# A hybrid decoder layer: the second parts of twelve weight splits, by accumulating transfers instead of GpSimd subtractions

## The chip, the cores and the metric

The kernel runs on one core of one Trainium2 chip. The metric is the device time of one execution in microseconds (us). The engines are PE (TensorE; PEld are its weight loads), DVE (VectorE), ACT (ScalarE), POOL (GpSimd) and SP (SyncE, which here only issues transfers). Transfers run on 16 DMA engines; SP, ACT and POOL can issue them.

## The reference

One decoder layer on 1024 tokens of width 1024, all in float32. A first projection of the normalised input is cut into the parts of four gated delta-rule heads (key, query, value of 128 columns each, an output gate `dz`, a decay and a beta for each token) and of four differential-attention heads. The outputs of both groups go through `w_out`, and a gated feed-forward block with a short causal convolution follows.

```python
proj = rms_norm(h, norm1_w[l]) @ w_in[l]
dq, dk, dv, dz, da, db, fq, fk, fv = jnp.split(proj, IN_SPLITS, axis=-1)
qkv = jax.nn.silu(causal_dwconv(jnp.concatenate([dq, dk, dv], axis=-1), dn_conv_w[l]))
...
o_a = gated_delta_rule(q_a, k_a, v_a, g_a, beta_a).astype(h.dtype)
o_a = rms_norm(o_a, dn_norm_w[l]) * jax.nn.silu(dz.reshape(B_, S_, DN_HEADS, DN_HEAD_V))
...
h = h + mix @ w_out[l]
u = causal_dwconv(rms_norm(h, norm2_w[l]) @ w_up[l], ffn_conv_w[l], ffn_conv_b[l])
gate, up = jnp.split(u, 2, axis=-1)
h = h + (jax.nn.silu(gate) * up) @ w_down[l]
```

## The kernel before, in words

PE multiplies in a reduced form of float32 (fp32r). To keep float32's accuracy every large operand x is split in two: the high part is x copied into that form, the low part is x minus the high part. A product is then three matmuls: high by high, high by low and low by high.

`split_w` (L200) makes the two parts of a tile of weights that has been loaded into a raw buffer (`raw`, three buffers in turn). ACT writes the high part (L202, `whi`), and then POOL (L204) or DVE (L206) subtracts it from the raw weights and writes the low part (`wlo`). Both parts come from one pool of five buffers (`wt`), which the splits take in turn: high, low, high, low, and so on. So a low part's buffer is the one that held the high part two splits earlier, and it comes free when PE has read that for the last time.

`gemm_T` (L415) computes one projection of a delta head, transposed: 128 columns of `w_in` against all 1024 tokens, in two halves of 512 tokens, each 8 times L422, L423 (high part of the weights) and L424 (low part), 48 matmuls in all. Its sums (`gT`, two PSUM buffers) are copied out by ACT at L433 (`pT`). `proj_T` (L429) calls it for the key (kind 1), the query (0) and the value (2) of each of the four heads. Key and query of head 0 are split earlier, while the input is normalised. `proj_nat` (L383 to L411) computes 256 columns untransposed; one call makes the second half of the gate, `dz`, from two raw tiles, each with four of the eight rows of blocks of the weights: L403 and L404 with the high parts, then L406 with the low parts.

The heads are worked one behind the other. While head h is prepared (`delta_prep`: decay `dec`, four-tap convolutions L573 with their activation L575, transposes `pk` L611 and `pv` L657, score products `pkk` and `pkq` L638, L639, which DVE masks at L643, L645), inverted (`delta_inverse`, L684 to L743) and scanned (`delta_scan`: `pP`, `pzz`, `pS`, `po`, with DVE steps `s` between them), PE fills its gaps with the projections of the next head. POOL has, beside the subtractions, causal masks (L594, L673), a product with the decay (L647) and one with the gate (`szh`, L791).

No order is written out by hand for this stage. A scheduler sets each engine's order when the program is built, from priorities given by `part(...)` and from its own estimates of durations; afterwards every engine runs its instructions strictly in that order, and an instruction that waits holds up all behind it. Transfers issued by SP stand in SP's order in the same way; a raw buffer's next load waits until its last reader is done.

Of the kernel before, what the change touches and what calls it, by code (L numbers as in the profile page):

```python
# [10 lines left out]
F32 = mybir.dt.float32  # L11
# [3 lines left out]
AF = mybir.ActivationFunctionType  # L15
ALU = mybir.AluOpType
AX = mybir.AxisListType

P = 128
# [39 lines left out]
def hybrid_layer(ctx, tc, x, positions, norm1_w, w_in, dn_conv_w, dn_a_log, dn_dt_bias,  # L59
# [2 lines left out]
                 ffn_conv_b, w_down, cst, out, dbg=None, stop=None):  # L62
    nc = tc.nc
    V, S, G, PE = nc.vector, nc.scalar, nc.gpsimd, nc.tensor
    dbg = dbg or {}

    cp = ctx.enter_context(tc.tile_pool(name="cp", bufs=1))
# [14 lines left out]
    @contextmanager  # L82
    def part(name):
        p = tc.cur_priority
        q = max(0, p - PRI[name])
        tc.cur_priority = q
        yield
        tc.cur_priority = p + tc.cur_priority - q
# [3 lines left out]
    def nm(s):  # L92
        uid[0] += 1
        return f"{s}_{uid[0]}"
# [4 lines left out]
    def gtr(s):  # L99
        return gt(s, dt=F32R)  # L100

    def jt(s, dt=F32):
        return jp.tile([P, T], dt, tag="j", name=nm(s))

    def ct_(s, dt=F32):
        return cq.tile([P, T], dt, tag="c", name=nm(s))
# [13 lines left out]
    def psG(s="pG"):  # L120
        return pq.tile([P, 512], F32, tag="G", name=nm(s), bufs=2)
# [16 lines left out]
    win = w_in.rearrange("l d c -> (l d) c")  # L138
# [61 lines left out]
    def split_w(raw, lo_eng=None, w=T, alloc=None):  # L200
        hi, lo = ((alloc or wt)(s)[:, 0:w] for s in ("whi", "wlo"))
        S.activation(hi, raw[:, 0:w], AF.Copy)  # L202
        if lo_eng is G:
            G.tensor_tensor(lo, raw[:, 0:w], hi.bitcast(F32), op=ALU.subtract)  # L204
        else:
            V.tensor_tensor(lo, raw[:, 0:w], hi.bitcast(F32), op=ALU.subtract)  # L206
        return hi, lo

    def load_w128(w, c0, lo_eng=None, after=None):

        raw = rp.tile([P, T], F32, tag="raw", name=nm("raw"))
        if after is not None:
            G.tensor_copy(raw[:, 0:1], after)
        nc.sync.dma_start(raw.rearrange("p (k c) -> p k c", c=P),
                          w[:, c0:c0 + P].rearrange("(k p) c -> p k c", p=P))
        hi, lo = split_w(raw, lo_eng)
        return (hi.rearrange("p (k c) -> p k c", c=P), lo.rearrange("p (k c) -> p k c", c=P))

    def load_wn(srcs, lo_eng=None, kg=4, alloc=None, after=None):


        wd = sum(w for _, _, w in srcs)
        parts = []
        for k0 in range(0, NK, kg):
            n = min(kg, NK - k0)
            raw = rp.tile([P, T], F32, tag="raw", name=nm("raw"))
            if after is not None:
                V.tensor_copy(raw[:, 0:1], after)
            rv = raw[:, 0:n * wd].rearrange("p (k c) -> p k c", c=wd)
            o = 0  # L230
            for w, c0, w_ in srcs:
                nc.sync.dma_start(
                    rv[:, :, o:o + w_],
                    w[k0 * P:(k0 + n) * P, c0:c0 + w_].rearrange("(k p) c -> p k c", p=P))
                o += w_
            hi, lo = split_w(raw, lo_eng, n * wd, alloc)
            parts.append((hi.rearrange("p (k c) -> p k c", c=wd),
                          lo.rearrange("p (k c) -> p k c", c=wd)))
        return lambda kt: (parts[kt // kg][0][:, kt % kg, :], parts[kt // kg][1][:, kt % kg, :])
# [39 lines left out]
    def new_xn():  # L279

        return [tuple(xp.tile([P, 4 * T], F32R, tag="xn", name=nm("xn")) for _ in range(2))
                for _ in range(2)]

    def xs(xn, part, kt, a, b):
        q = a // 512
        return xn[q][part][:, kt * 512 + a - q * 512:kt * 512 + b - q * 512]
# [13 lines left out]
    xn = new_xn()  # L300
# [3 lines left out]
    with tc.manual_schedule(engines={mybir.EngineType.Activation}):  # L304
        for tt in range(NT + 1):
# [7 lines left out]
            if 0 < tt < 4:  # L313
                k = tt - 1
                n = min(3, NK - 3 * k)
                hi, lo = (gtr("w0")[:, 0:n * 264].rearrange("p (k c) -> p k c", c=264) for _ in range(2))
# [70 lines left out]
    def proj_nat(srcs, dst, lo_eng=None, extra=None):  # L387


        wf = load_wn(srcs, lo_eng, 4) if extra is None else lambda kt: tuple(t[:, kt % 3, :] for t in srcs[kt // 3])  # L390
        npt = 1 if extra is not None else 2
        for q in range(2):
            st = jt("pn")
            for t0 in range(0, 4, npt):
                ps = psG("pn")
                for i in range(npt):
                    tt = q * 4 + t0 + i
                    a, b = tt * P, tt * P + P
                    w = 264 if extra is not None else 256
                    o = ps[:, i * w:(i + 1) * w]  # L400
                    for kt in range(NK):
                        wh, wl = wf(kt)
                        PE.matmul(o, xs(xn, 0, kt, a, b), wh, start=kt == 0, stop=False)  # L403
                        PE.matmul(o, xs(xn, 1, kt, a, b), wh, start=False, stop=False)  # L404
                    for kt in range(NK):
                        PE.matmul(o, xs(xn, 0, kt, a, b), wf(kt)[1], start=False, stop=kt == NK - 1)  # L406
                if extra is not None:
                    V.tensor_copy(extra[:, tt, :], ps[:, 256:264])
                S.activation(st[:, t0 * 256:(t0 + npt) * 256], ps[:, 0:npt * 256], AF.Copy)
                yield  # L410
            nc.sync.dma_start(  # L411
                pn_dram[q * 512:(q + 1) * 512, dst:dst + 256].rearrange("(t p) c -> p t c", p=P),
                st.rearrange("p (t c) -> p t c", c=256))

    def gemm_T(w, c0, x_, ps, lo_eng, qq=(0, 1)):  # L415

        whi, wlo = pre.pop(c0 // P, None) or load_w128(w, c0, lo_eng)
        for q in qq:
            qs = (q * 512, q * 512 + 512)
            o = ps(q)  # L420
            for kt in range(NK):
                PE.matmul(o, whi[:, kt, :], xs(x_, 0, kt, *qs), start=kt == 0, stop=False)  # L422
                PE.matmul(o, whi[:, kt, :], xs(x_, 1, kt, *qs), start=False, stop=False)  # L423
                PE.matmul(o, wlo[:, kt, :], xs(x_, 0, kt, *qs), start=False, stop=kt == NK - 1)  # L424
            yield q, o
# [3 lines left out]
    def proj_T(h, kind):  # L429
        ct = kind * 4 + h  # L430
        st = praw[ct] = ct_("pT")
        for q, o in gemm_T(win, ct * P, xn, lambda q: psG("gT"), G):
            S.activation(st[:, q * 512:(q + 1) * 512], o, AF.Copy)  # L433
            yield

    def steps(gen, n=99):
        for _ in range(n):
            if next(gen, gen) is gen:
                break

    nat0 = proj_nat(wf0, 0, extra=dab)
    head0 = [proj_T(0, kind) for kind in (1, 0, 2)]
    steps(nat0, 4)
    steps(head0[0], 1)
# [18 lines left out]
    for bits in (8, 8, 8):  # L463
        e = math.floor(math.log2(abs(rest)))
        q = 2.0 ** (e - bits + 1)
# [115 lines left out]
    def load_rows(h):  # L581
        dec = gt("dec")
        nc.sync.dma_start(dec, G_dram[h:h + 1, :].broadcast_to([P, T]))
        return dec
# [387 lines left out]
    def delta_proj(h):  # L972
        for kind in (1, 0, 2):
            steps(proj_T(h, kind))

    def delta_end(d):
        with part("dscan"):
            delta_scan(d)
        with part("dout"):
            delta_out(d)  # L980

    ds_ = []
    for h in range(4):
        dec = load_rows(h)
        if h > 0:
            with part("dproj"):
                delta_proj(h)
            if h == 3:
                with part("dz1"):
                    steps(proj_nat([(win, 1792, 256)], 256, G))  # L990
        with part("dprep"):
            ds_.append(delta_prep(h, dec))
        if h > 0:
            delta_end(ds_[h - 1])
        with part("dinv"):
            delta_inverse(ds_[h])
# [15 lines left out]
    def load_wo(k0, c, eng, alloc=None):  # L1012

        parts = []
        for i in range(2):
            raw = rp.tile([P, T], F32, tag="raw", name=nm("raw"))
            r0 = (k0 + 2 * i) * P
            nc.sync.dma_start(raw.rearrange("p (k c) -> p k c", c=512),
                              wout[r0:r0 + 2 * P, c * 512:(c + 1) * 512].rearrange("(k p) c -> p k c", p=P))
            parts.append(split_w(raw, eng, T, alloc))  # L1020
        return lambda k: tuple(t[:, (k % 2) * 512:(k % 2) * 512 + 512] for t in parts[k // 2])
# [379 lines left out]
```

## Time and profile before

| | us |
|---|---|
| median of 3 runs | 1429.41 (1425.66 to 1430.79) |
| the profiled execution | 1430.1 |
| its span, first to last instruction | 1428.4 |
| PE busy in the span | 1334.5 |
| DVE, ACT, POOL busy | 878.3, 611.3, 377.0 |

The profiled execution is 0.7 us above the median of the runs. Busy times are sums over the whole span; since the stages of the kernel have different limits, a change in one stage is read from that stage's rows. In a row with square brackets, the bracket holds the time that the engine sat idle just before, and the instruction whose end released it. PE's clock is the one that the chip granted, as a share of full speed.

### The profile page before, as it was taken

The numbers are of one execution on the slowest core, as the hardware profiler recorded it, in microseconds if no ns is written. First come the engines' busy times: TensorE is split into PE (matmuls) and PEld (weight loads), VectorE is DVE, ScalarE is ACT, GpSimd is POOL, SyncE is SP. The second block draws the span as 40 slices with busy tenths as digits, with TensorE's granted clock in tenths as the row PEclk, the third lists the DMA queues.
The fourth block names the chain that finished last, engine by engine and source line by source line (L and its number), as shares of the span: only waits on it lengthen the run. The fifth ranks groups of instructions, "written<-read, shape, count | busy, mean of one in ns | idle before, by whom it ended". The sixth has DMA issues, their size and how long they took to land. (4 is left out here: it accounts for less than half of the span.)

```text
span 1428.4 us, 20608 instructions
## 1 busy us (share of the span) xinstructions
PE 1334.5 (93%) x7927; PEld 1126.6 (79%) x7927; DVE 878.3 (61%) x1745; ACT 611.3 (43%) x1086; POOL 377.0 (26%) x295
## 2 busy tenths in 40 slices
PE   7998898989989998999887999999999989999998
PEld 6876676888989986778665788888888868888887
DVE  5467978886342368867787666666666656334321
ACT  6445454533325365665554444444444435222220
POOL 3044313131242245240022434444333420000000
PEclk8999999999999999999998999999999999999999
DMA  7231112031543267455331222222222247547421
GB/s 225 83 80 35 34 39 75 17 113 66 162 109 116 88 169 192 105 134 162 123 121 29 89 74 89 85 78 89 89 74 82 82 137 243 195 149 229 139 88 59
DMA packets 143393, 155.14 MB, mean 109 GB/s; under 512 B 9279, under 2 KB 114367, under 8 KB 143295
## 3 DMA queue, kind: packets, MB, share of 16 engines
q1 hardware_dynamic: 130815, 144.14, 31.8%
q0 software_dynamic: 11008, 8.39, 3.1%
q8 instruction: 62, 1.02, 0.3%
q10 hardware_dynamic: 1472, 1.29, 0.3%
q14 instruction: 36, 0.29, 0.1%
HBM read 111.32 MB, written 38.29 MB: 105 GB/s over the span
## 5 line engine op out<-in xcount | busy, mean ns | idle before, releaser
L385 PE MATMUL pd<-whi,gl 128*128 128x512 f32 x352 | 137.0, 389 | 0.0
L383 PE MATMUL pd<-whi,gh 128*128 128x512 f32 x352 | 137.0, 389 | 0.0
L384 PE MATMUL pd<-wlo,gh 128*128 128x512 f32 x352 | 137.0, 389 | 0.0
L204 POOL TENSOR_TENSOR wlo<-raw,whi 128x1024 fp32r<-128x1024 f32 x34 | 83.8, 2471 | 194.1 <-PE gT L424 68.2
L1316 POOL TENSOR_TENSOR acc<-acc,acc 128x1024 f32<-128x1024 f32 x22 | 53.6, 2437 | 243.8 <-issue 215.5
L403 PE MATMUL pn<-whi,xn 128*128 128x256 f32 x448 | 116.3, 293 | 0.0
L404 PE MATMUL pn<-whi,xn 128*128 128x256 f32 x448 | 115.4, 291 | 0.0
L1339 ACT ACTIVATE gh<-act 128x1024 fp32r<-128x1024 f32 x42 | 44.6, 1061 | 123.9 <-PE pd L384 100.2
L1340 DVE TENSOR_TENSOR gl<-act,gh 128x1024 fp32r<-128x1024 f32 x42 | 52.0, 1241 | 68.9 <-ACT gh L1339 68.6
L403 PEld LDWEIGHTS pn<-whi,xn 128*128 128x128 f32 x448 | 87.3, 195 | 0.3
L404 PEld LDWEIGHTS pn<-whi,xn 128*128 128x128 f32 x448 | 87.0, 195 | 0.1
L202 ACT ACTIVATE whi<-raw 128x1024 fp32r<-128x1024 f32 x58 | 61.0, 1052 | 52.1 <-issue 18.3
L206 DVE TENSOR_TENSOR wlo<-rx,whi 128x1024 fp32r<-128x1024 f32 x22 | 28.9, 1315 | 82.6 <-ACT whi L202 82.3
L424 PE MATMUL gT<-xn,wlo 128*128 128x512 f32 x192 | 79.3, 413 | 0.0
L1230 PE MATMUL pa<-xT,whi 128*128 128x512 f32 x176 | 70.5, 400 | 9.3 <-ACT xT L1103 5.3
L422 PE MATMUL gT<-xn,whi 128*128 128x512 f32 x192 | 78.8, 410 | 0.0
L423 PE MATMUL gT<-xn,whi 128*128 128x512 f32 x192 | 78.6, 409 | 0.0
L202 ACT ACTIVATE whi<-rx 128x1024 fp32r<-128x1024 f32 x22 | 23.3, 1061 | 127.4 <-POOL rx L1271 127.4
L383 PEld LDWEIGHTS pd<-whi,gh 128*128 128x128 f32 x352 | 66.1, 188 | 13.8
L385 PEld LDWEIGHTS pd<-whi,gl 128*128 128x128 f32 x352 | 66.1, 188 | 13.7
L384 PEld LDWEIGHTS pd<-wlo,gh 128*128 128x128 f32 x352 | 66.1, 188 | 13.6
L206 DVE TENSOR_TENSOR wlo<-raw,whi 128x1024 fp32r<-128x1024 f32 x24 | 29.4, 1225 | 72.3 <-PE pd L384 53.1
(377 smaller groups left out, 3765.9 us busy)
## 6 DMA issues: line engine op xcount, KB each, us to landing
act<-act_dram SPq DMA_DIRECT2D x42, 512.0 KB, 4.5
rw<-in_w_up_dram SPq DMA_DIRECT2D x22, 512.0 KB, 3.8
act_dram<-acc SPq DMA_DIRECT2D x22, 512.0 KB, 2.6
raw<-in_w_down_dram SPq DMA_DIRECT2D x22, 512.0 KB, 4.4
raw<-in_w_in_dram SPq DMA_DIRECT2D x18, 512.0 KB, 4.0
pn_dram<-pn SPq DMA_DIRECT2D x16, 512.0 KB, 3.4
rx<-in_w_up_dram SPq DMA_DIRECT2D x22, 256.0 KB, 2.8
rz<-in_w_up_dram SPq DMA_DIRECT2D x22, 256.0 KB, 3.3
```

Of the source, the lines that this page charges most:

```text
L202: S.activation(hi, raw[:, 0:w], AF.Copy)
L204: G.tensor_tensor(lo, raw[:, 0:w], hi.bitcast(F32), op=ALU.subtract)
L206: V.tensor_tensor(lo, raw[:, 0:w], hi.bitcast(F32), op=ALU.subtract)
L383: PE.matmul(ps, lh, rh, start=first, stop=False)
L384: PE.matmul(ps, lh, rl, start=False, stop=False)
L385: PE.matmul(ps, ll, rh, start=False, stop=last)
L403: PE.matmul(o, xs(xn, 0, kt, a, b), wh, start=kt == 0, stop=False)
L404: PE.matmul(o, xs(xn, 1, kt, a, b), wh, start=False, stop=False)
L422: PE.matmul(o, whi[:, kt, :], xs(x_, 0, kt, *qs), start=kt == 0, stop=False)
L423: PE.matmul(o, whi[:, kt, :], xs(x_, 1, kt, *qs), start=False, stop=False)
L424: PE.matmul(o, wlo[:, kt, :], xs(x_, 0, kt, *qs), start=False, stop=kt == NK - 1)
L1230: PE.matmul(ps, wh[:, ks], xh[k], start=first, stop=False, skip_group_check=not start)
```

## The change

`split_w` gets a third way to make the low part: ACT writes the negated high part into the low part's buffer (a copy with scale -1), and a transfer issued by POOL adds the raw weights to it where they lie. `proj_T` and the projection of the gate's second half choose it. `proj_T`'s choice applies to ten projections: the value of head 0 and all three of heads 1 to 3; key and query of head 0 have been split before, by a call that still names POOL. With the gate's two tiles that is twelve splits. All others keep their engine.

```diff
+    DMA = nc.sync
...
     def split_w(raw, lo_eng=None, w=T, alloc=None):
         hi, lo = ((alloc or wt)(s)[:, 0:w] for s in ("whi", "wlo"))
         S.activation(hi, raw[:, 0:w], AF.Copy)
-        if lo_eng is G:
+        if lo_eng is DMA:
+
+            S.activation(lo, raw[:, 0:w], AF.Copy, scale=-1.0)
+            G.dma_start(lo.bitcast(F32), raw[:, 0:w], accum_op=ALU.add)
+        elif lo_eng is G:
             G.tensor_tensor(lo, raw[:, 0:w], hi.bitcast(F32), op=ALU.subtract)
...
-        for q, o in gemm_T(win, ct * P, xn, lambda q: psG("gT"), G):
+        for q, o in gemm_T(win, ct * P, xn, lambda q: psG("gT"), DMA):
...
-                    steps(proj_nat([(win, 1792, 256)], 256, G))
+                    steps(proj_nat([(win, 1792, 256)], 256, DMA))
```

`DMA` is only a name for the choice; the transfers are issued by POOL. Lines behind the edit are five higher in the changed kernel (L422 is L427 there).

The scheduler's orders move with it. On ACT, where head 0's value is split and head 1's key begins, the order before was this (`gT` and `pT` are the projections of head 0; the numbers tell buffers apart):

```order
L433 ACTIVATE pT_98_545<-gT_107_710 128x512 [waits PE_49]
L202 ACTIVATE whi_153_1251<-raw_152_1249 128x1024 [waits DMAHW7_49,Pool_49]
L790 ACT_TABLE_LOAD
L790 ACTIVATE szh_256_1707<-szh_256_1707 128x1024 [waits DMAHW4_49]
L790 ACTIVATE szh_373_2398<-szh_373_2398 128x1024 [waits DMAHW5_49]
L433 ACTIVATE pT_103_628<-gT_108_736 128x512 [waits PE_49]
L202 ACTIVATE whi_159_1310<-raw_158_1308 128x1024 [waits DMAHW1_49,Pool_49]
L433 ACTIVATE pT_109_762<-gT_113_769 128x512 [waits PE_49]
L433 ACTIVATE pT_109_762<-gT_114_795 128x512 [waits PE_49]
```

On ACT at the same place now:

```order
L206 ACTIVATE wlo_112_766<-raw_110_763 128x1024 [waits PE_49,Pool_49]
L438 ACTIVATE pT_98_545<-gT_107_710 128x512 [waits PE_49]
L203 ACTIVATE whi_153_1252<-raw_152_1250 128x1024 [waits DMAHW7_49]
L795 ACT_TABLE_LOAD
L795 ACTIVATE szh_256_1711<-szh_256_1711 128x1024 [waits DMAHW4_49]
L795 ACTIVATE szh_373_2405<-szh_373_2405 128x1024 [waits DMAHW5_49]
L438 ACTIVATE pT_103_628<-gT_108_736 128x512 [waits PE_49]
L206 ACTIVATE wlo_154_1253<-raw_152_1250 128x1024 [waits Pool_49]
L203 ACTIVATE whi_159_1312<-raw_158_1310 128x1024 [waits DMAHW1_49]
L438 ACTIVATE pT_109_762<-gT_113_770 128x512 [waits PE_49]
L206 ACTIVATE wlo_160_1313<-raw_158_1310 128x1024 [waits PE_49,Activation_49]
L438 ACTIVATE pT_109_762<-gT_114_796 128x512 [waits PE_49]
```

Three copies into low parts' buffers have come in, each with the wait for that buffer, ahead of evacuations of projections.

On PE, at the first transposes `pk` of head 0's key, which stand between matmuls of head 1's query (`gT_162`), the order before was this:

```order
L422 MATMUL gT_162_1340<-xn_16_140,whi_159_1310 128x512
L423 MATMUL gT_162_1340<-xn_17_141,whi_159_1310 128x512
L424 MATMUL gT_162_1340<-xn_16_140,wlo_160_1311 128x512
L422 MATMUL gT_162_1340<-xn_16_140,whi_159_1310 128x512
L611 MATMUL pk_123_933<-k_sb_96,acc_118_918 128x128 [waits Activation_49]
L611 MATMUL pk_123_933<-k_sb_96,acc_118_918 128x128 x3
L611 MATMUL pk_124_943<-k_sb_96,acc_118_918 128x128 x4
```

On PE at the same place now:

```order
L427 MATMUL gT_162_1343<-xn_16_140,whi_159_1312 128x512 [waits Activation_49]
L428 MATMUL gT_162_1343<-xn_17_141,whi_159_1312 128x512
L429 MATMUL gT_162_1343<-xn_16_140,wlo_160_1313 128x512
L427 MATMUL gT_162_1343<-xn_16_140,whi_159_1312 128x512
L428 MATMUL gT_162_1343<-xn_17_141,whi_159_1312 128x512
L616 MATMUL pk_123_934<-k_sb_96,acc_118_919 128x128 [waits Activation_49]
L616 MATMUL pk_123_934<-k_sb_96,acc_118_919 128x128 x3
L616 MATMUL pk_124_944<-k_sb_96,acc_118_919 128x128 x4
```

Ten matmuls of `gT_162` stood ahead of the transposes, and five stand there now; the other five follow behind them.

On PE, at the first low parts of the gate's second half (`wlo_405` is the first tile's, `wlo_408` the second's; `pz0` belongs to the inverse of head 2), the order before was this:

```order
L406 MATMUL pn_410_2820<-wlo_405_2810,xn_14_138 128x256 x4
L406 MATMUL pn_410_2820<-wlo_408_2816,xn_14_138 128x256 [waits Pool_49]
L406 MATMUL pn_410_2820<-wlo_408_2816,xn_14_138 128x256
L702 MATMUL pz0_379_2519<-inv1_376_2426 32x32 [waits DVE_49]
L702 MATMUL pz0_379_2519<-inv1_376_2426 32x32 x31
L406 MATMUL pn_410_2820<-wlo_408_2816,xn_14_138 128x256 x2
```

On PE at the same place now:

```order
L411 MATMUL pn_410_2832<-wlo_405_2820,xn_14_138 128x256 [waits DMASW2_49]
L707 MATMUL pz0_379_2526<-inv1_376_2433 32x32 [waits DVE_49]
L707 MATMUL pz0_379_2526<-inv1_376_2433 32x32 x31
L411 MATMUL pn_410_2832<-wlo_405_2820,xn_14_138 128x256 x3
L411 MATMUL pn_410_2832<-wlo_408_2827,xn_14_138 128x256 [waits DMASW3_49]
L411 MATMUL pn_410_2832<-wlo_408_2827,xn_14_138 128x256 x3
```

The small products of the inverse have moved ahead of the second tile's low part, and the waits are now for transfers (`DMASW`).

## Rows read from the trace of the kernel before

**Rows 1.** The page's first part: busy us, share of the span, instructions.

```profile
PE 1334.5 (93%) x7927; PEld 1126.6 (79%) x7927; DVE 878.3 (61%) x1745; ACT 611.3 (43%) x1086; POOL 377.0 (26%) x295
```

**Rows 2.** Stages: length, busy us by engine (instructions), PE's clock, DMA share, GB/s.

```profile
120.00:150.00 30.00, 23.46 (x113) 19.03 (x112) 28.65 (x69) 14.81 (x31) 13.88 (x11) 0.96 0.18 54
...
240.00:270.00 30.00, 24.41 (x137) 19.90 (x135) 26.11 (x95) 13.21 (x24) 9.41 (x9) 0.94 0.17 49
```

**Rows 3.** POOL in time: start, us, line, out<-in, count [idle before].

```profile
69.30 2.46 POOL L204 TENSOR_TENSOR wlo<-raw,whi 128x1024 fp32r<-128x1024 f32 x1 [32.90 <-PE gT L424]
...
85.62 2.40 POOL L204 TENSOR_TENSOR wlo<-raw,whi 128x1024 fp32r<-128x1024 f32 x1 [5.16 <-PE gT L424]
...
118.97 2.36 POOL L204 TENSOR_TENSOR wlo<-raw,whi 128x1024 fp32r<-128x1024 f32 x1 [15.02 <-PE gT L424]
...
264.73 2.40 POOL L204 TENSOR_TENSOR wlo<-raw,whi 128x1024 fp32r<-128x1024 f32 x1 [9.01 <-PE gT L423]
```

**Rows 4.** DVE in time, same columns.

```profile
86.34 1.73 DVE L544 TENSOR_TENSOR ekd<-Gl,Gc 128x32 f32<-128x32 f32 x1
87.99 0.27 DVE L539 COPY setup<-pg 32x128 f32<-32x128 f32 x1
...
119.25 2.12 DVE L186 SCALAR_TENSOR_TENSOR r<-rt,r 128x16 f32<-128x16 f32 x1
...
130.51 0.17 DVE L186 SCALAR_TENSOR_TENSOR r<-rt,r 128x16 f32<-128x16 f32 x1
...
264.94 2.33 DVE L687 TENSOR_TENSOR inv<-inv 128x120 f32<-128x120 f32 x1
```

**Rows 5.** The convolution's line L573: count, ns min/median/max, first to last start.

```profile
L573 DVE SCALAR_TENSOR_TENSOR acc<-pT,dcw,acc x36: 1268/1279/3433, 98.4 to 302.9; 128x1023 f32<-128x1023 f32 x12, 128x1022 f32<-128x1022 f32 x12, 128x1021 f32<-128x1021 f32 x12
```

**Rows 6.** PE in time, the groups that it idled before.

```profile
109.90 1.97 PE L611 MATMUL pk<-k_sb,acc 128*128 128x128 f32 x8 [5.08 <-ACT acc L575]
...
122.10 1.16 PE L639 MATMUL pkq<-acc,acc 128*128 128x128 f32 x8 [1.54 <-DVE dec L645]
...
146.88 1.17 PE L611 MATMUL pk<-k_sb,acc 128*128 128x128 f32 x8 [3.21 <-ACT acc L575]
...
159.28 0.94 PE L639 MATMUL pkq<-acc,acc 128*128 128x128 f32 x6 [1.68 <-DVE dec L645]
...
246.11 0.49 PE L758 MATMUL pzz<-s,U 128*128 128x128 f32 x2 [2.15 <-DVE s L756]
...
267.58 0.49 PE L766 MATMUL pS<-s,kn 128*128 128x128 f32 x2 [1.74 <-DVE s L762]
```

**Rows 7.** Slices of 2 us, columns as in rows 2.

```profile
148.00:150.00 2.00, 2.00 (x7) 1.52 (x6) 1.79 (x9) 2.00 (x16) 0.00 (x0) 0.50 0.00 0
...
248.00:250.00 2.00, 2.00 (x11) 2.00 (x11) 1.24 (x7) 0.37 (x1) 0.00 (x0) 0.50 0.49 145
```

**Rows 8.** ACT by line, 60 to 270 us: count, busy us, mean ns, idle.

```profile
L202 ACT ACTIVATE whi<-raw 128x1024 fp32r<-128x1024 f32 x12 | 12.6, 1050 | 0.0
```

**Rows 9.** Transfers by line: issuing queue, count, KB each, median us to landing.

```profile
raw<-in_w_in_dram SPq DMA_DIRECT2D x18, 512.0 KB, 4.0
...
mhl<-mT POOLq DMA_DIRECT2D x16, 256.0 KB, 5.3
K<-K POOLq DMA_DIRECT2D x32, 128.0 KB, 4.3
```

**Rows 10.** POOL and DVE in time, at two of POOL's issues.

```profile
538.72 1.56 POOL L1038 DMA_DIRECT2D mhl<-mT  x2
...
538.92 0.17 DVE L184 SCALAR_TENSOR_TENSOR qrt<-qrs 128x16 f32<-128x16 f32 x1
```

**Rows 11.** PE in time, matmuls that read low parts first.

```profile
75.03 0.39 PE L424 MATMUL gT<-xn,wlo 128*128 128x512 f32 x1
...
97.39 0.39 PE L424 MATMUL gT<-xn,wlo 128*128 128x512 f32 x1
...
271.99 0.87 PE L406 MATMUL pn<-wlo,xn 128*128 128x256 f32 x6
```

## The prediction

> **What bounds the kernel now.** I read the page's busy times first, then busy time by stage, then the engines' rows in time for the 200 us in which the changed splits run. PE is busy for 93% of the span [rows 1]; what can be won is the time in which PE waits. In the stage of the delta heads that is a lot: between 120 and 150 us PE is busy for 23.46 of 30 us while DVE is busy for 28.65, and between 240 and 270 us it is 24.41 against 26.11 [rows 2]. The reader is to see that DVE's chain (convolutions, decay, inverse, scan) sets the pace there, and that the projections of the next head only fill PE's gaps.
>
> What slows DVE is the next thing to read. A low part made on POOL takes 2.4 us [rows 3], and whenever one runs, the DVE instruction beside it stretches until it ends. L186 on 16 columns takes 0.17 us alone, and 2.12 us from 119.25, while POOL subtracts from 118.97 to 121.33 [rows 3, 4]. L687 from 264.94 takes 2.33 us and ends with the subtraction that began at 264.73 [rows 3, 4]. The convolution step L573 has a median of 1.28 us and a maximum of 3.43 us [rows 5]. So a subtraction on POOL costs a busy DVE 2 to 2.2 us, and the time ahead of six PE groups names DVE, or an ACT instruction that waited for DVE, as the releaser [rows 6].
>
> **The change part by part.** It touches 12 splits, each one 128x1024: one for the value of head 0 (call it v0), nine for heads 1 to 3 in the order key, query, value (k1 to v3), two for the second half of the gate (dz0, dz1). Twelve POOL subtractions go. Twelve ACT instructions come, which write the negated high part into the low part's buffer, and twelve transfers issued by POOL, which add the raw weights to it.
>
> *Relief of DVE, where PE waits for it.* I count only what PE idles today, because elsewhere PE is full. The gap of 5.08 us before 109.90 ends with the activation of the convolved key of head 0. Its convolutions run beside v1's subtraction: 3.43 - 1.28 = 2.15 us. The same chain begins with the decay of head 0, which is copied out at 87.99, behind an instruction of 1.73 us that waited for q1's subtraction [rows 4]; against 0.17 us for a small one that is 1.56 us, and I take 1.1, because PE's transpose for that copy runs in the same time (an estimate). Together 3.25. The gap before 122.10 holds k2's stretched L186: DVE gets 1.95 back, PE can win no more than its 1.54. Before 146.88 stand convolutions again: 2.15 of 3.21. Before 159.28: 1.68, before 246.11: 2.15, before 267.58: 1.74, each no larger than the 2 us or so that DVE gets back [rows 6]. Sum: 3.25 + 1.54 + 2.15 + 1.68 + 2.15 + 1.74 = 12.5 us. For k3, q3 and v3 I count nothing, since PE has no gap behind them. From below the relief could be half of this, if PE's gaps close for another reason late; from above it is 12.5, the gaps themselves.
>
> *Clock.* After two of these gaps the granted clock is 0.50, the 1.2 GHz level: from 148 to 150 and from 248 to 250 us [rows 7]. In such a slice PE does half of its work, so 1 us goes in each. With the gaps closed I take 1.7 us for both, between 0 and 3.4.
>
> *The new way of a low part.* Before: 2.4 us on POOL. Now: one ACT instruction, 1.05 us like L202 [rows 8], then a transfer of X us from issue to landing. No transfer here adds, so X is bounded: below by a plain 512 KB load, 4.0 us; above by twice the 5.3 us of POOL's 256 KB transfers, 10.6 us, since this one reads two operands of 512 KB [rows 9]. I take 7, nearer to POOL's own two rows (4.3 us for 128 KB, 5.3 for 256 KB), which add about 1 us for each doubling, plus 0.7 for the second operand. The Trainium skill's "DMA: Bandwidth & Descriptors", section "Anatomy of one DMA — SWDGE (gpsimd) path", gives 2.0 us plus the bytes at 436 GB/s, which would be an estimate of 3.2 us for 512 KB; by that no low part would be late, and the sum would be -12.2 us instead of -8.4; no run here shows it, and POOL's 128 KB already take 4.3.
>
> Most of the twelve have cover: the buffer comes free when PE ends the projection two before, and PE then has a whole projection of 48 matmuls to do, or far more beside the scan. Two have not. **v0**: its buffer is released at 69.30 [rows 3], so the transfer is issued at about 70.4 and lands at 77.4; PE's first matmul on it stands at 75.03 [rows 11]. PE waits 2.4 us, and the gates' matmul behind it in PE's order shifts with it, so this wait is on the path. **dz1**: released at 264.73 [rows 3], issued at 265.8, landed at 272.8. Before, its first matmul is the fifth of the group at 271.99 [rows 11], at about 272.5; with the gap of 1.74 gone and one small group moved ahead of it, 271.4. PE waits 1.4 us. The next closest is q1: released at 85.62 by the end of v0's projection [rows 3], issued at 86.7, needed at 97.39 [rows 11]: it holds up to X = 10.7. Cost of the waits: 2.4 + 1.4 = 3.8 us.
>
> *ACT.* 12 x 1.05 = 12.6 us more, on an engine that is busy for about half of each of these stages [rows 2]. The wait for a free buffer passes from POOL, where little stood behind it, to ACT, where the evacuation of the projection, the next high part and the scan's instructions stand behind it. In nine of the twelve places the evacuation next in the row waits for the end of the same projection anyway, so the wait itself costs next to nothing and the 1.05 us fall into ACT's idle time. I take 2.0 us for what does not, between 0 and 5.
>
> *POOL and SP.* An issue takes 0.78 us of POOL, half of 1.56 for two [rows 10]. SP's loads of raw weights now wait for the landing instead of the subtraction, 5 us later; the raw buffers are three, and their next readers are a projection or more away. Nothing counted.
>
> **Sum.** -12.5 - 1.7 + 3.8 + 2.0 = -8.4 us. Against the profiled execution, 1430.1 us (span 1428.4): 1421.7. The median of the runs, 1429.41, is 0.7 lower: **1421 us**.
>
> **The rivals.** *Slow additions* (ends slower). If the adding transfer takes 15 us, v0 waits 10.4, dz1 9.4 and q1 4.3 us: -12.2 + 24.1 = +11.9, 1441 us. It breaks even at X = 11.2 (twice X less 22.4 is zero), just above my bound, and reaches 0.5% at 13.4. For it: nothing here adds in a transfer. Against: 512 KB land in 4.0 us [rows 9], and 15 us would be nearly four such loads. Chance 0.12.
>
> *The lock was not what PE waited for.* Half of the relief and no clock: -6.2 + 3.8 + 2.0 = -0.4, 1429 us. For it: other POOL work stays (masks, the products with the decay and the gate), ACT gets longer in the same chain, and the order on PE before the key's transposes has five matmuls fewer to cover the gap. Against: the stretched instructions end with the subtractions to within 0.1 us. This covers the case that the change doesn't do what it says, with the issue of the transfer holding DVE as the subtraction did. Chance 0.28.
>
> *The issue starves.* DVE could hold the transfer's issue up in its turn. The two issues from 538.72 take 1.56 us together and DVE's small instruction beside them keeps 0.17 us [rows 10], but none of DVE's long ones stood there. With 2.5 us more at v0 and dz1: -8.4 + 5.0 = -3.4, 1426 us. The Trainium skill's page "SBUF — State Buffer", section "SBUF: two separate sides", states this: a busy DVE can keep POOL from writing descriptors, 620 ns becoming 3100. That rule speaks against the change, and [rows 10] don't bear it out. Chance 0.10.
>
> **How the numbers follow.** Forecast 0.50, with 1413 (all terms at their good ends: -12.5 - 3.4, no waits) to about 1425 inside it. About 0.08 of that lies within 0.5%, which is about what a measurement of this kernel can tell from no change; of the two middle rivals some 0.08 lie beyond it on the fast side. Faster 0.50, same 0.37, slower 0.13. The range of 8 in 10 runs from 1412, the good end, to 1433, which takes in the two middle rivals and leaves out slow additions.
>
> **What would show it.** Right: no DVE instruction of 2 us in the stage but those beside the remaining POOL work; PE's gaps before the second pair of score products (122.10 now) and before the scan steps at 246 and 267 gone; a clock of 1.00 after the key's transposes of head 1. X is read from the issue rows; a wait of PE for the adding transfer at v0's first low matmul of X - 4.6 us. Wrong: X above 11, PE groups waiting for ACT instructions that queue behind the negation, or gaps of the old size with another releaser.

## The result, and the profile after

The changed kernel takes 1417.76 us (median of 4 runs, 1415.33 to 1419.08), the kernel before 1428.01 in the same company: 0.992 of it, 95% interval 0.9893 to 0.9947. Timed a second time, it came to 1417.07 us and 0.9922 (0.9907 to 0.9937). That is 11 us saved, where 8.4 were forecast from the profiled execution. The profiled execution took 1419.08 us, its span is 1417.1 us.

Three rows of the view by stage, after (columns as in [rows 2]; the last row takes in all of the delta heads), and the last row of before for comparison:

```profile
120.00:150.00 30.00, 26.06 (x132) 21.00 (x132) 27.72 (x92) 20.54 (x51) 9.18 (x11) 1.00 0.31 71
240.00:270.00 30.00, 29.36 (x346) 25.40 (x344) 26.07 (x85) 16.95 (x31) 2.78 (x4) 1.00 0.23 54
...
60.00:340.00 280.00, 259.27 (x2329) 218.73 (x2328) 202.47 (x618) 142.61 (x319) 62.42 (x62) 0.98 0.32 84
```

```profile
60.00:340.00 280.00, 249.50 (x2186) 209.19 (x2184) 218.95 (x597) 130.26 (x302) 82.96 (x62) 0.96 0.19 56
```

From 60 to 340 us PE is busy 9.8 us more and DVE 16.5 us less; ACT has 12.4 us more, about its twelve copies of 1.05 us. (The changed kernel is further on at 340 us, so the two windows do not hold quite the same work.) DVE in time, after, shows why (start, us, line, out<-in, [idle before]):

```profile
97.85 8.09 DVE L578 SCALAR_TENSOR_TENSOR acc<-pT,dcw,acc 128x1023 f32<-128x1023 f32 x6
...
116.42 0.16 DVE L187 SCALAR_TENSOR_TENSOR r<-rt,r 128x16 f32<-128x16 f32 x1
...
119.53 1.69 DVE L186 TENSOR_TENSOR rt<-rt,u 128x16 f32<-128x16 f32 x1
121.14 1.27 DVE L578 SCALAR_TENSOR_TENSOR acc<-pT,dcw,acc 128x1022 f32<-128x1022 f32 x1
```

and POOL after, beside the last two of them:

```profile
118.78 2.40 POOL L652 TENSOR_TENSOR acc<-acc,eg 128x1024 f32<-128x1024 f32 x1 [15.50 <-PE pkq L644]
121.14 0.88 POOL L207 DMA_DIRECT2D wlo<-raw  x1
```

The small step that took 2.12 us [rows 4] takes 0.16 now. What still stretches (L186, 1.69 us) ends with a two-operand product that was left on POOL. The convolution that begins together with the issue of a transfer keeps its 1.27 us.

PE after, the groups that it idled before, which answer to [rows 6], with v0's first low part ahead of them:

```profile
75.83 0.50 PE L429 MATMUL gT<-xn,wlo 128*128 128x512 f32 x1 [0.37 <-DMA wlo<-raw]
107.23 1.39 PE L616 MATMUL pk<-k_sb,acc 128*128 128x128 f32 x8 [2.60 <-ACT acc L580]
126.64 1.09 PE L662 MATMUL pv<-k_sb,acc 128*128 128x128 f32 x8 [2.11 <-ACT acc L580]
141.87 1.09 PE L616 MATMUL pk<-k_sb,acc 128*128 128x128 f32 x8 [1.41 <-ACT acc L580]
...
243.95 0.49 PE L763 MATMUL pzz<-s,U 128*128 128x128 f32 x2 [0.64 <-DVE s L761]
```

The gaps before the score products (122.10 and 159.28 before) and before the scan step of 267 are gone, and those of the key's transposes are about half. The transfers, by line (issuing queue, count, KB, median us from the start of the issue to the landing), and the issues on POOL (min/median/max ns):

```profile
wlo<-raw POOLq DMA_DIRECT2D x12, 512.0 KB, 4.5
```

```profile
L207 POOL DMA_DIRECT2D wlo<-raw x12: 847/876/1049, 70.8 to 255.1; - x12
```

### The profile page after: what moved, and what is told of

The parts are those of the page before. It is cut to its first block, busy times and chain, and to the rows that moved or that the text cites. A ratio compares the mean times of both kernels' runs of the same rounds, so it can differ in the third digit from the quotient of the medians.

```text
span 1417.1 us, 20633 instructions
## 1 busy us (share of the span) xinstructions
PE 1332.3 (94%) x7927; PEld 1125.1 (79%) x7927; DVE 854.8 (60%) x1745; ACT 622.0 (44%) x1098; POOL 355.9 (25%) x295
## 5 line engine op out<-in xcount | busy, mean ns | idle before, releaser
L408 PE MATMUL pn<-whi,xn 128*128 128x256 f32 x448 | 116.3, 293 | 0.0
L409 PE MATMUL pn<-whi,xn 128*128 128x256 f32 x448 | 115.2, 291 | 0.0
L408 PEld LDWEIGHTS pn<-whi,xn 128*128 128x128 f32 x448 | 86.8, 194 | 0.4
L409 PEld LDWEIGHTS pn<-whi,xn 128*128 128x128 f32 x448 | 86.6, 194 | 0.1
L427 PE MATMUL gT<-xn,whi 128*128 128x512 f32 x192 | 78.4, 408 | 0.0
L209 POOL TENSOR_TENSOR wlo<-raw,whi 128x1024 fp32r<-128x1024 f32 x22 | 52.5, 2398 | 91.3 <-ACT whi L203 34.8
L1235 PE MATMUL pe<-x,whi 128*128 128x512 f32 x176 | 69.8, 397 | 2.8 <-ACT cu L1294 2.8
```

What stands on the lines that cost most here:

```text
L1235: PE.matmul(ps, wh[:, ks], xh[k], start=first, stop=False, skip_group_check=not start)
```

## The experiments

All ratios are to the kernel before, timed beside each on the same chip. "The changed kernel" stands at 0.9922 (0.9907 to 0.9937).

### POOL's subtraction back, in the changed kernel's order

```diff
-            G.dma_start(lo.bitcast(F32), raw[:, 0:w], accum_op=ALU.add)
+            G.tensor_tensor(lo, raw[:, 0:w], hi.bitcast(F32), op=ALU.subtract)
```

> The changed kernel with one line put back: behind ACT's negated copy POOL subtracts into the same buffer, as before, in the place of the adding transfer. Every engine's order of instructions is that of the changed kernel, so only what POOL does at the twelve places differs. Theory (POOL's subtraction holds DVE up, and PE waits for DVE): the relief is lost and the copies on ACT stay; DVE again shows instructions of about 2.2 us beside the subtractions, PE's gaps come back, 1427 to 1432 us, at least 9 above the changed kernel. Rival (what gained was the new order, with fewer matmuls ahead of the transposes and the loads moved): it stays within 3 us of the changed kernel, 1416 to 1421 us.

Measured: 1435.47 us, 1.0045 (1.0028 to 1.0062). DVE and PE in time in this kernel:

```profile
97.60 10.27 DVE L578 SCALAR_TENSOR_TENSOR acc<-pT,dcw,acc 128x1023 f32<-128x1023 f32 x6
...
124.15 3.47 DVE L578 SCALAR_TENSOR_TENSOR acc<-pT,dcw,acc 128x1022 f32<-128x1022 f32 x1
```

```profile
109.16 1.97 PE L616 MATMUL pk<-k_sb,acc 128*128 128x128 f32 x8 [5.26 <-ACT acc L580]
131.84 1.92 PE L662 MATMUL pv<-k_sb,acc 128*128 128x128 f32 x8 [4.27 <-ACT acc L580]
```

With every engine's order the same, subtractions in the place of the twelve transfers cost 0.0123 of 1428 us, 17.6 us. The six convolution steps take 10.27 us instead of 8.09, and the gap before the key's transposes is back at 5.26. PE's gaps of more than 0.15 us between 60 and 340 us add up to 30.9 us, against 20.3 in the changed kernel. The granted clock withheld 15.4 us there against 6.8 (worked out further down), which is part of the rest. The new order is no gain by itself: with the copies on ACT and the subtraction behind them, it lies 6.4 us above the kernel before. One reason shows in the rows above: a subtraction that stood beside a 16-column step before now meets a convolution (3.47 us from 124.15), which the value's transposes wait for.

### One operand or two on POOL

```diff
-            S.activation(lo, raw[:, 0:w], AF.Copy, scale=-1.0)
+            S.activation(lo, raw[:, 0:w], AF.Copy, scale=-2.0)
+            G.tensor_tensor(lo, lo.bitcast(F32), hi.bitcast(F32), op=ALU.add)
             G.dma_start(lo.bitcast(F32), raw[:, 0:w], accum_op=ALU.add)
```

> The changed kernel with twelve additions of two operands on POOL (128x1024, the size of the old subtraction), each ahead of its transfer: ACT writes twice the negated part, POOL adds the high part to it, the transfer adds the raw weights, and the low part comes out the same. Theory (a POOL instruction that reads two operands holds DVE up): the relief of DVE is lost though the transfers stay, 1430 to 1437 us, like the kernel with POOL's subtraction in the transfer's place (1435.5). Rival (what made that kernel slow was something else than DVE held up by POOL): 1418 to 1422 us, the low parts being 2.4 us later.

The second kernel keeps ACT's copy at scale -1.0 and has this in the place of the addition:

```diff
+            G.tensor_scalar(lo, lo.bitcast(F32), 1.0, None, op0=ALU.mult)
```

> As the kernel with twelve spare additions on POOL, and in the same order on every engine, but POOL's instruction reads one operand (a product of the 128x1024 tile with 1.0, in place). Theory (only POOL's instructions with two operands hold DVE up: in the changed kernel six convolution steps took 8.08 us beside POOL's one-operand mask, and 10.23 us beside the subtraction before): at least 6 us below the kernel with two operands, 1418 to 1424 us. Rival (any POOL instruction of 128x1024 holds DVE up): within 2 us of the two-operand kernel, 1430 to 1437 us.

Measured: 1439.36 us with two operands, 1.0084 (1.0057 to 1.011); 1427.73 with one, 1.0 (0.9984 to 1.0016). POOL and the convolution beside it, first with two operands:

```profile
128.84 2.39 POOL L206 TENSOR_TENSOR wlo<-wlo,whi 128x1024 fp32r<-128x1024 f32 x1
...
128.84 3.47 DVE L578 SCALAR_TENSOR_TENSOR acc<-pT,dcw,acc 128x1022 f32<-128x1022 f32 x1
```

then with one:

```profile
124.10 2.77 POOL L206 TENSOR_SCALAR wlo<-wlo 128x1024 fp32r<-128x1024 f32 x1
...
124.07 2.14 DVE L578 SCALAR_TENSOR_TENSOR acc<-pT,dcw,acc 128x1022 f32<-128x1022 f32 x1
```

The two kernels have one order on all engines and are 12 us apart, as expected: two operands cost the convolution 2.2 us, one operand, though 0.4 us longer on POOL, 0.9. The expected level was missed: one operand was to give 1418 to 1424 us. The waits of PE for transfers in that kernel (us in total, times, longest) show 6.2 us of the rest. Its order also differs from the changed kernel's, and no run prices that.

```profile
PE pn L411 <- DMA wlo<-raw: 3.2, 1, 3.2
PE gT L429 <- DMA wlo<-raw: 3.0, 1, 3.0
```

These two are dz1 and v0, the places named as uncovered, now that their low parts come 2.8 us later.

### What the transfers themselves cost

```diff
-            G.dma_start(lo.bitcast(F32), raw[:, 0:w], accum_op=ALU.add)
```

> The changed kernel without the twelve adding transfers: the low part is left as ACT's negated copy, so that part of the products is wrong. Theory: the transfer costs PE the one wait of 0.37 us at v0, so 1417 us, within 2 of the changed kernel's 1417.8. Rival (the transfers cost elsewhere too: they share the DMA engines with the loads, and POOL's issues hold DVE): 1413 us or less.

```diff
-            G.dma_start(lo.bitcast(F32), raw[:, 0:w], accum_op=ALU.add)
+            G.dma_start(lo[0:16].bitcast(F32), raw[0:16, 0:w], accum_op=ALU.add)
```

> The changed kernel with each adding transfer cut to the first 16 of 128 partitions (64 KB of 512), so that the rest of the low part is left as ACT's negated copy and the products are wrong. Every engine's order is that of the changed kernel, which the kernel without the transfers did not keep: it came out at 1411.0 us. Theory (the transfer as such costs PE only the wait of 0.37 us at v0, and the 6.8 us by which the kernel without it is faster are its other order): 1416.5 to 1418.5 us. Rival (the transfers' traffic or their lateness slows PE or DVE): 1411 to 1413 us.

Measured: 1410.99 us without transfers, 0.9878 (0.9861 to 0.9895); 1413.15 with 16 rows, 0.9894 (0.9872 to 0.9917). The first fell on the rival's side, the second at the rival's edge. My theory said that the kernel with 16 rows would not gain; it lies 4.0 us under the changed kernel by the ratios, though the intervals overlap. The changed kernel was run again for this:

> The changed kernel itself, unaltered, timed in the company of the next kernels and looked at a second time. Theory: 1416 to 1419 us, and the same gaps of PE in the stage of the delta heads; where the granted clock drops may differ. If the transfers' traffic cost something, as the kernel with 16 rows (1413.2 us) leaves open, this run stays above that kernel by more than 2 us; if the distance of 4.6 us was chance, it comes closer than 2.

Measured: 1417.07 us; the distance stays over 2 us. The gaps of PE did not all stay the same: before the key's transposes of head 0 PE waited 3.07 us instead of 2.60, before those of head 1 not at all instead of 1.41. The traces show one place where the transfers cost time. The first decay's load, which the key's convolutions of head 0 wait behind, runs at the same time as q1's transfer. Transfers between 84 and 96 us, in the changed kernel:

```profile
wlo<-raw POOLq DMA_DIRECT2D x1, 512.0 KB, 4.9
dec<-G_dram SPq DMA_DIRECT2D x1, 512.0 KB, 6.0
```

and with 16 rows:

```profile
dec<-G_dram SPq DMA_DIRECT2D x1, 512.0 KB, 4.8
wlo<-raw POOLq DMA_DIRECT2D x1, 64.0 KB, 3.0
```

DVE's first step on the decay waits for ACT, which waits for that load, in the changed kernel and with 16 rows:

```profile
96.71 1.23 DVE L597 TENSOR_TENSOR dec<-dec,Gc 128x1024 f32<-128x1024 f32 x1 [6.96 <-ACT eg L596]
```

```profile
96.64 1.23 DVE L597 TENSOR_TENSOR dec<-dec,Gc 128x1024 f32<-128x1024 f32 x1 [5.79 <-ACT eg L596]
```

The key's transposes are then waited for 1.42 us with 16 rows, against 2.60 and 3.07 in the two profiled executions of the changed kernel, where the load took 6.0 and 6.5 us:

```profile
107.16 1.09 PE L616 MATMUL pk<-k_sb,acc 128*128 128x128 f32 x8 [1.42 <-ACT acc L580]
```

After 2.60 the granted clock falls to the 1.2 GHz level, after 1.42 it stays. Slices of 2 us, changed kernel, then 16 rows:

```profile
108.00:110.00 2.00, 2.00 (x7) 1.71 (x7) 0.69 (x1) 2.00 (x17) 0.00 (x0) 0.50 0.99 243
110.00:112.00 2.00, 2.00 (x10) 1.57 (x9) 0.69 (x1) 0.67 (x3) 0.00 (x0) 0.68 0.73 281
```

```profile
108.00:110.00 2.00, 2.00 (x12) 1.55 (x11) 0.69 (x1) 2.00 (x18) 0.00 (x0) 1.00 1.00 358
110.00:112.00 2.00, 2.00 (x14) 1.43 (x13) 0.69 (x1) 1.97 (x14) 0.00 (x0) 1.00 0.02 6
```

So in these two executions a longer gap (1.2), a clock drop (2 x 0.50 + 2 x 0.32 = 1.6) and v0's wait (0.4) come to 3.2 us. From v0's issue (70.81 against 72.61 with 16 rows) to the wait of PE that ends at 326.26 against 324.56, the changed kernel loses 3.5 us to the other. What the transfers cost in the median is less certain, since the 4.0 us rest on intervals that overlap and the clock drops elsewhere differ between executions. How much of the 6.3 us of the kernel without transfers is its other order stays open.

### One part alone

The first kernel has POOL in the gate's second half again, the second has it in the projections again:

```diff
-                    steps(proj_nat([(win, 1792, 256)], 256, DMA))
+                    steps(proj_nat([(win, 1792, 256)], 256, G))
```

> The projections by transfers, the gate's second half by POOL as before. Theory (each gap of PE behind a subtraction is a gain of its own): the two gaps at the scan steps come back, 1.5 + 1.7 us and about 1 us of clock, so about 4 us above the changed kernel, 1422 us. Rival (the scan's gaps later on grew in the changed kernel, so that the gate's share was given back): 1417 to 1419 us.

```diff
-        for q, o in gemm_T(win, ct * P, xn, lambda q: psG("gT"), DMA):
+        for q, o in gemm_T(win, ct * P, xn, lambda q: psG("gT"), G):
```

> The gate's second half by transfers, the projections by POOL as before. Theory: about 4 us below the kernel before, 1424 us. Rival (the gate's share was given back by the scan's later gaps): 1427 to 1429 us. With the projections-only kernel the two gains should add up to the 10.2 us of the whole change, within 2 us.

Measured: projections only 1419.27 us, 0.9939 (0.9918 to 0.9961), so 8.7 us; gate only 1424.99, 0.9985 (0.9971 to 0.9999), so 2.1. The parts add up to the whole, 10.8 against 11.1. The sum came out as expected. Of the parts, the projections came out at the rival's edge (1419) and not at the theory's 1422; the gate is worth about 2 us rather than the 4 expected, and its interval ends just below no gain at all. With the projections only, one of the two gaps is back (2.38 us before a scan step at 238.00, beside a subtraction from 234.95), the other in part (1.15 us before a scan step at 259.06, behind a subtraction from 255.92).

### DVE in POOL's place

The kernel before, with the twelve subtractions on DVE:

```diff
-        for q, o in gemm_T(win, ct * P, xn, lambda q: psG("gT"), DMA):
+        for q, o in gemm_T(win, ct * P, xn, lambda q: psG("gT"), V):
...
-                    steps(proj_nat([(win, 1792, 256)], 256, DMA))
+                    steps(proj_nat([(win, 1792, 256)], 256, V))
```

> The kernel before with the same twelve subtractions on DVE in the place of POOL: no copy on ACT, no transfer. Theory (POOL's subtraction costs a busy DVE about 2.2 us, its own subtraction costs it 1.31 us): DVE gets back 0.9 us at each of the places where PE waits for it, some 8 of 12, and ACT is spared; between the two kernels, 1418 to 1424 us. Rival (DVE sets the pace, and the subtraction now stands in its order wherever the scheduler puts it, ahead of what PE waits for): 1427 to 1433 us.

Measured: 1418.83 us, 0.9933 (0.9916 to 0.995): no different from the changed kernel. DVE's row (min/median/max ns):

```profile
L211 DVE TENSOR_TENSOR wlo<-raw,whi x12: 1209/1222/3474, 68.7 to 242.5; 128x1024 fp32r<-128x1024 f32 x12
```

At 1.22 us, the engine that sets the pace does the work for less than the 2 us and more that POOL's help costs it where the two collide. (The one of 3.47 us ran beside POOL's product for the gate.) Part of the gain is lost again at one place, a gap of 5.95 us of PE before 295.60, behind a subtraction that POOL still makes for the attention heads.

### The attention heads' splits as well

By transfers:

```diff
-        return proj_nat([(win, 3080 + pr * 256, 256)], 1536 + pr * 256, G)
+        return proj_nat([(win, 3080 + pr * 256, 256)], 1536 + pr * 256, DMA)
```

and the same for their queries and keys.

> The changed kernel with the twelve splits of the attention heads' projections done by adding transfers as well. Theory (the relief is worth something only where PE waits for DVE beside a subtraction): between 349 and 630 us of the changed kernel one such gap stands behind two subtractions, 5.19 us before 418.1, where POOL subtracts from 410.8 to 415.5; 3 to 5 us of it go, 1413 to 1415 us. Rival (each split is worth the 0.85 us that it was worth in the delta heads, wherever it stands): 1407 to 1409 us. Other rival (the transfers now meet the attention's loads, which PE waits for in places, 2.44 us before 403): 1418 us or more.

Measured: 1441.68 us, 1.0082 (1.006 to 1.0104): about 23 us slower than the changed kernel by the ratios, on the last rival's side and far beyond it. PE's waits between 340 and 520 us in it:

```profile
PE pn L411 <- DMA wlo<-raw: 17.5, 8, 4.3
```

A pair issued at 487.95 and 489.87 held PE until 498.29; the second landed 8.4 us after its issue. Here PE comes to the low parts about 2 us after the high ones (16 matmuls of L408 and L409, 0.12 us apart), and ACT's copy had itself waited for the buffer that PE was still reading. So the late transfer of the prediction's first rival came true here, by short cover and by second transfers that took 6.8 to 8.4 us instead of 4.5.

By DVE instead, for their queries and keys too, first on top of the changed kernel, then with DVE in all twenty-four places:

```diff
-        return proj_nat([(win, 3080 + pr * 256, 256)], 1536 + pr * 256, G)
+        return proj_nat([(win, 3080 + pr * 256, 256)], 1536 + pr * 256, V)
```

> The changed kernel with the attention heads' twelve subtractions moved from POOL to DVE. Theory (the gap of 5.19 us before 418.1, behind two subtractions on POOL that hold DVE for 4.7 us, shrinks by the 2 us that two subtractions on DVE cost less; no transfer is waited for): 1414 to 1417 us. Rival (DVE's twelve subtractions, 15.7 us in all, stand ahead of the softmax steps that PE waits for): 1419 us or more.

> All twenty-four subtractions, of the delta heads, the gate and the attention heads, on DVE; no copy on ACT, no transfer. Theory: the sum of the two kernels with DVE in one stage each, so 1 to 4 us below the kernel that has DVE in the delta heads only, 1415 to 1422 us. Rival (DVE is too full to take them in both): above the kernel before, 1428 us.

Measured: 1405.37 us, 0.9836 (0.9819 to 0.9853), and 1407.2 us, 0.9849 (0.9827 to 0.9871). Both beat the changed kernel by 10 to 12 us, far more than expected, and the two intervals overlap. The changed kernel ahead of its 5.19 us gap, POOL, DVE and PE:

```profile
410.80 4.74 POOL L209 TENSOR_TENSOR wlo<-raw,whi 128x1024 fp32r<-128x1024 f32 x2
```

```profile
410.86 2.48 DVE L861 TENSOR_TENSOR sqk<-qk,sn 128x128 f32<-128x128 f32 x1 [2.71 <-POOL qk L851]
413.26 2.42 DVE L862 TENSOR_TENSOR sqk<-qk,sn 128x128 f32<-128x128 f32 x1
```

```profile
418.10 1.97 PE L883 MATMUL pT<-k_sb,stk 128*128 128x128 f32 x8 [5.19 <-DVE stk L874]
```

The same place with DVE subtracting:

```profile
403.25 0.29 DVE L861 TENSOR_TENSOR sqk<-qk,sn 128x128 f32<-128x128 f32 x1 [2.73 <-POOL qk L851]
403.46 0.28 DVE L862 TENSOR_TENSOR sqk<-qk,sn 128x128 f32<-128x128 f32 x1
403.67 1.22 DVE L211 TENSOR_TENSOR wlo<-raw,whi 128x1024 fp32r<-128x1024 f32 x1
```

```profile
407.47 1.09 PE L883 MATMUL pT<-k_sb,stk 128*128 128x128 f32 x8 [0.64 <-DVE stk L874]
```

That place gives 4.6 us. The other one, which I had not counted, is the scan between 290 and 316: two subtractions of POOL, from 293.34 and 299.53, stretched DVE steps of the next head's inverse to 2.2 and 2.3 us there, and from the step at 292.09 (290.04 with DVE) to the one at 316.00 (310.21) it is 3.7 us shorter. The remaining 4 us are not placed; clock drops may be part of them, and how many there are changes between executions of one kernel (below).

## Why the prediction was right, point by point

The total was about right, -11 against -8.4, and so was the mechanism; the terms were not all of the right size, and the errors partly cancelled. The signs that it named came true in the main: the gaps before 122.10 and 267 are gone and the one before 246 is down to 0.64 us, and the instructions of DVE that still take about 2 us between 60 and 340 us all stand beside POOL's remaining work, the decay's mask among it.

- **Relief of DVE, -12.5.** The six gaps of [rows 6] (a seventh, of 1.78 us before 130.98, was not counted) sum to 15.4 us. Their counterparts are 2.60, 0, 1.41, 0, 0.64 and 0, so 10.75 came back; in the second profiled execution they are 3.07, 0, 0, 0, 0.64 and 0, so 11.7. In the first, the 5.08 gave 2.5 and not 3.25, because the chain from head 0's decay was held by the decay's load beside q1's transfer, as the 16-row kernel shows; the gap before 146.88 gave 1.8 and not 2.15, and the one before 246 gave 1.5 of 2.15. All of PE's gaps above 0.15 us between 60 and 340 us add up to 30.2 us before and to 20.3 and 18.4 after, so what the prediction left out stayed about as it was. That POOL's subtraction was the cause is shown by the kernel with it put back: 17.6 us in the same order.
- **Which DVE instructions are held.** The prediction says that the DVE instruction beside a subtraction always stretches. The rows of before show that this is too wide. Beside the subtraction from 196.98 to 199.36 two scan steps that read PSUM (`pS`, `pP`) keep their 0.35 us:

```profile
196.98 2.38 POOL L204 TENSOR_TENSOR wlo<-raw,whi 128x1024 fp32r<-128x1024 f32 x1 [9.99 <-PE gT L423]
```

```profile
197.41 0.35 DVE L771 SCALAR_TENSOR_TENSOR s<-s,egl,pS 128x128 f32<-128x128 f32 x1 [0.58 <-PE pS L766]
198.33 0.35 DVE L756 SCALAR_TENSOR_TENSOR s<-pP,egn,nv 128x128 f32<-128x128 f32 x1 [0.58 <-PE pP L754]
```

The scan's gaps at 246 and 267 came from steps of the next head's inverse (L681, L687) that stand in DVE's order between the scan's, and whose tiles lie in SBUF. The prediction counted nothing for this subtraction (q3), so its sum does not suffer.
- **Clock, -1.7.** Between 60 and 340 us, time times one minus the granted clock, over slices of 2 us, sums to 10.3 us before and to 6.8 and 11.9 us in the two profiled executions of the changed kernel. The forecast drops at 148 and 248 are gone in the first, but a drop is not tied to a gap closely enough to be counted ahead. The term can't be confirmed.
- **Waits for the adding transfer, +3.8.** This was the term that was mis-sized: X is 4.5 us (up to 5.0), not 7, near the lower bound, the plain load's 4.0 [rows 9]. By X - 4.6 v0, whose transfer took 5.0, had to wait 0.4 us and waited 0.37. dz1 did not wait, but it was close: its transfer, issued at 255.10, landed 4.8 us later, as PE came to it. With X = 5.0 the prediction's own sum is -12.5 - 1.7 + 0.4 + 2.0 = -11.8 us, near the 11 measured. What the prediction did not see is that the transfers hold up other loads: the slower load of the decay cost 1.2 us (counted above, in the relief that fell short), and a clock drop of 1.6 us stood behind it.
- **ACT, +2.0.** No gap of PE ends with a copy into a low part, or with an instruction that stood behind one for long. The copies and the new order together cost 6.4 us where POOL's subtraction follows them; where a transfer follows, their share can't be told from the order's.
- **The sum.** Without the clock, the terms came to about -10.4 (relief -10.75, waits +0.4) against the -6.7 forecast for relief, waits and ACT together. The relief was put 0.8 to 1.8 us too high, the waits 3.4 too high and ACT's price has not been seen, so the errors partly cancelled; that the total missed by less than 3 us is partly luck.
- **The rivals.** Slow additions: 4.5 us, far from the 11.2 at which it decided (11.0 with q1's wait, which that figure leaves out). That DVE did not wait for POOL: excluded by the subtraction put back. The starved issue: the twelve issues took 0.85 to 1.05 us, [rows 10] having 0.78, and the four beside convolutions took 0.85 to 0.91. The Trainium skill's "SBUF — State Buffer", section "SBUF: two separate sides", gives its numbers for a transfer issued by GpSimd, about 620 ns alone and 3100 beside a `tensor_copy` of VectorE. No copy out of SBUF stood beside the twelve issues, so this kernel neither confirms nor refutes it.
- **The price of a transfer by the notes.** The Trainium skill's "DMA: Bandwidth & Descriptors", section "Anatomy of one DMA — SWDGE (gpsimd) path", gave the estimate of 3.2 us; 4.5 were measured for a transfer that adds, and up to 8.4 behind another one. The measurement decides: the estimate was 1.3 us too low, my 7 was 2.5 too high.

## What to carry to other kernels

In this kernel an elementwise instruction of two operands on GpSimd held a convolution or sum of VectorE on SBUF tiles for about as long as it ran; steps that read PSUM kept their time. Where VectorE is in the chain that TensorE waits for, count such an instruction as VectorE's own work. The first thing to try is VectorE itself (1.2 us here against 2.2 lost); a copy on ScalarE with an adding transfer came out the same, and only where the reader is 6 us or more away (1.05 for the copy, 4.5 to 5 from the start of the issue to the landing) and no other transfer or load that is waited for is under way. A single profile doesn't settle 2 or 3 us: compare kernels that have the same order on all engines.

## What the runs showed of the hardware that was not expected

- A transfer that adds 512 KB onto 512 KB lands in 4.5 us, against 4.0 for a plain load of the same size; when a second one was issued 1.9 us after the first, it took 8.4. A 512 KB load of the decay took 6.0 and 6.5 us beside such a transfer, 4.8 beside one of 64 KB.
- Beside a one-operand POOL instruction of 2.77 us a convolution step that began with it takes 2.14 us, beside a two-operand one of 2.39 us 3.47, alone 1.27. One that began at 157.91, 1.8 us into a one-operand instruction, took 1.27.
- The time that the clock withheld between 60 and 340 us (worked out as above) can differ between two executions of one kernel by more than some of the changes here are worth: 6.8 and 11.9 us in the changed kernel, though the spans are only 1.9 us apart. The others, one execution each: 3.4 without transfers, 5.2 with 16 rows, 10.3 before, 15.4 with the subtraction put back.
